# A third weight tile, and weights asked for earlier, in a two-layer decoder trunk on one core

## The chip, the cores and the metric

One core of a Trainium2 chip runs the whole program as one launch. The metric is the device time of one execution in microseconds. Before the change it is 1894.92 us, the median of 3 runs (1894.47 to 1899.17).

## The reference

The input is 512 tokens of width 1024 in float32. Two layers each do a half-weighted gated feed-forward step, a token mixer, and a second half-weighted feed-forward step; a final norm ends the program.

```python
def swiglu(x, w_gate, w_up, w_down):
    return (jax.nn.silu(x @ w_gate) * (x @ w_up)) @ w_down      # hidden width 2816

for i in range(DEPTH):                                          # 2 layers
    h = h + 0.5 * swiglu(rmsnorm(h, ffn_norm_a[i]), ffn_a_w_gate[i], ffn_a_w_up[i], ffn_a_w_down[i])
    m = rmsnorm(h, mix_norm[i])
    h = h + (mla_mixer(m, ...) if i % 2 == 0 else nsa_mixer(m, ...))
    h = h + 0.5 * swiglu(rmsnorm(h, ffn_norm_b[i]), ffn_b_w_gate[i], ffn_b_w_up[i], ffn_b_w_down[i])
return rmsnorm(h, final_norm)
```

The mixer of layer 0 is latent attention (`mla_mixer`): queries, keys and values come through low-rank projections, 16 heads, with a rotary part. The mixer of layer 1 is sparse attention (`nsa_mixer`): 16 heads in 4 groups; each token attends in a compressed branch (keys and values pooled over blocks of 32 tokens), a selected branch and a window branch, and the three outputs are summed with learned gates. All is causal.

## The kernel before, in words

Every matrix is split into a high and a low part (a copy in the faster matmul type, then source less copy), and a product is three matmuls: high x high, high x low, low x high (`mm3`, L161). So each slab of weights is loaded by SyncE's queue into a raw tile `wr`, copied by ScalarE into the high half of a weight tile `w`, and subtracted by VectorE, or in attention by GpSimd (`lo_pool`, L147 to L150), into the low half. `wslab` (L133) does all this; `wtiles` (L126) hands out the weight tiles, of which there are two in turn, and raw tiles are two as well. The high and low halves of a weight tile do not begin at its start: `wtiles` puts an offset of 0, 16 or 48 floats ahead of the high half and 0 or 32 more between the two, by the kind of use.

A pool's tiles lie in on-chip memory one behind the other, and the pools too: a scratch that the launch reserves, constants, the residual stream `h`, the normed activations (`x`, and `four` for tiles four times as wide), the weights (two weight tiles, a small tile, two raw tiles), a small pool, and then the pools of the current stage, feed-forward or attention.

The feed-forward stage (`ffn`, L369) does its first three hidden blocks plainly: gate and up products of 256-token halves (`plain`, L357, tiles `pg` and `pu`). The other 19 blocks form sums of weights and of activations and so need 7 products in place of 8 (`wsums` L309, `product` L348; tiles `px`, `pq`, `pg`, 256 wide). The down products (`pd`, 512 wide) run between them in units of three blocks, and the last one or two blocks (`tail`) at the end, where the next stage's norm is prepared. The norm's scale is applied late: gates and products are multiplied by a `row` that is computed from a sum of squares (`sumsq`, `norm_col`, `norm_bcast`) while the plain blocks run.

Latent attention (`mla`, L642) and sparse attention (`nsa`, L834) run a software pipeline over tiles of scores (`attend`, L569): scores on TensorE, softmax on VectorE and ScalarE, division by the sum on GpSimd (L772, L1091), transposes of the probabilities four tiles later, and the product with the values two or three tiles after that. Projections for later heads are cut into pieces and put into this pipeline by a table: `make(g, q, k, q2, c)` (L1190) gives the tile numbers at which the pieces of a group's first query, its keys, its second query, and the three steps of its compressed branch are issued. Of these three, `scores` forms the scores, `softmax` transposes them (`ptc`, L1041), normalises them, with the last scaling on GpSimd (`e`, L1053), and `turn` transposes them back (`ptc`, L1058).

A scheduler decides the order on each engine from the order of the code and priorities; each engine then works through its own list in order and waits on semaphores.

Of the kernel before, what the change touches and what calls it, by code (L numbers as in the profile page):

```python
# [18 lines left out]
P = 128  # L19
# [31 lines left out]
PAD = 16  # L51
TILES = 24
# [10 lines left out]
class Kern:  # L63
# [62 lines left out]
    def wtiles(self, kind="x"):  # L126

        t = self.first or self.wp.tile([P, 2048 + 3 * PAD], F32R, tag=f"w{self.nw % 2}", name="w")
        self.nw, self.first = self.nw + 1, None
        o, d = {"x": (0, 0), "act": (3 * PAD, 0), "half": (PAD, 2 * PAD)}[kind]  # L130
        return t[:, o : o + 1024], t[:, o + d + 1024 : o + d + 2048]
# [142 lines left out]
    def norm_col(self, n, s2, pool=False):  # L274
# [5 lines left out]
        return self.rsqrt_col(pc[:, 0:4], n, pool)  # L280
# [88 lines left out]
    def ffn(self, idx, gain_next, ap, tp):  # L369
        nc, a = self.nc, self.a  # L370
        self.scr, self.fp = (tp, "sq", 1), tp
        ah, al, ht, row = {}, {}, [], None
# [56 lines left out]

        gates = [self.bank("T", "pg") for _ in range(PLAIN)]  # L430
        for f, g in enumerate(gates):
            u = tu[f] = self.bank(("mm", "S")[f % 2], "pu")
            self.plain(idx, f, 0, g)
            if f == 1 and idx == 0:

                squares(0)
                tokens(3)
                squares(1)
            if f == 2:
                pb = self.norm_bcast(col)  # L440
                row = tp.tile([P, S], F32, tag="row", bufs=1, name="row")
                nc.scalar.activation(row, pb, AF.Copy)
                for e in range(2):
                    gate(e, gates[e])
                    act(e)
            self.plain(idx, f, 1, u)
            if f == 0 and idx:
                for c in self.late:
                    self.sumsq(self.h[c])
                col = self.norm_col(D, self.s2)  # L450
            elif f == 1 and idx == 0:
                squares(2)
                squares(3)
                col = self.rsqrt_col(sums, D)
            elif f == 2:
                gate(f, g)
                act(f)
            for p in (((0,), (1,), (2, 3)) if idx else ((0, 1), (2,), (3,)))[f]:
                self.combine(p)
# [182 lines left out]
    def mla(self, gain_next):  # L642
        nc, tc, a = self.nc, self.tc, self.a
        with ExitStack() as cx:
# [130 lines left out]
            def end(h):  # L775
# [58 lines left out]
    def nsa(self, gain_next):  # L834
        nc, tc, a = self.nc, self.tc, self.a
        with ExitStack() as cx:
# [18 lines left out]
            def pieces(src, done, more, nk=4):  # L855

                p, w = [], []

                def piece(k0):
                    if k0 == 0:  # L860
                        w.extend(self.wslab(src, (KC, P)))
                        p.append(self.mm_bank("pp"))
# [5 lines left out]
                return [partial(piece, k0) for k0 in range(0, KC, KC // nk)] + more  # L868

            def keys(g):  # L870
# [3 lines left out]
                def done(p):  # L874
                    tt.append(qp.tile([P, S], F32, tag="t", bufs=1, name="t"))
# [23 lines left out]
            def vals():  # L899

                ws = []

                def piece(j, kk):
                    if not ws:
                        ws.extend(self.wslab(a["nsa_w_v"][z], (4, 256), "half") for z in range(2))
# [9 lines left out]
                return [partial(piece, j, kk) for j in range(4) for kk in range(2)]  # L915

            def query(t2):
# [3 lines left out]
                def done(p):  # L921
                    tt.append(qp.tile([P, S], F32, tag="t", bufs=1, name="t"))
# [13 lines left out]
            with tc.tile_pool(name="cmp", bufs=1, reuse_waits="tile") as bp:  # L936
# [48 lines left out]
                for f in kf[:2]:  # L985
                    f()
# [5 lines left out]
                for f in kf[2:]:  # L992
# [149 lines left out]
            def end(h, z, br):  # L1142
# [12 lines left out]
                o, t = bank[m], tp.tile([P, S], F32, tag="p", bufs=6, name="ot")[0:64, :]  # L1155
# [15 lines left out]
            def w_o(c2):  # L1171

                w = []

                def piece(e):
                    if e == 0:
                        w.append(self.wslab(a["nsa_w_o"][0, c2], (2, 4, P), "act"))
                    self.w_o1(w[0], oh[:4], ol[:4], c2 + KP * e, e, False)

                return [partial(piece, e) for e in range(2)]  # L1180
# [153 lines left out]
```

## Time and profile before

| | |
|---|---|
| median of 3 runs | 1894.92 us |
| profiled execution | 1895.84 us, its span 1894.1 us |
| TensorE (PE) busy | 1865.5 us, 98% |
| weight loads into TensorE (PEld) | 1695.8 us, 90% |
| VectorE (DVE) busy | 1527.9 us, 81% |
| ScalarE (ACT) busy | 1088.9 us, 57% |
| GpSimd (POOL) busy | 244.7 us, 13% |
| granted TensorE clock, mean | 0.998 |
| read from memory | 178.96 MB, 96 GB/s over the span |

In the span's course, feed-forward runs from 0 to about 350 us, latent attention to about 550, feed-forward of both layers to about 1235, sparse attention to about 1530, and feed-forward to the end. Matmuls overlap each other, so the mean length of one (its latency) is longer than the distance between two starts; where a group's mean length rises, so does that distance. A list of waits names the engine's instruction, what released it, the total in us, how often and the longest. In a row of groups the numbers behind the first bar are busy us and mean ns, behind the second the idle time of the engine just before.

### The profile page before, as it was taken

To read this page: it belongs to the slowest core of one execution; us is meant where nothing else is said; L and a number is where in the kernel's file an instruction comes from. 1 tells how busy PE (TensorE), PEld (TensorE's weight loads), DVE (VectorE), ACT (ScalarE), POOL (GpSimd) and SP (SyncE) were. 2 spreads that over 40 slices of the span, in tenths; PEclk is the share of its full clock that TensorE was granted. 3 is DMA by queue.
4 is the path that set the end of the run, shared out by engine and by line. 5 is a ranking of instruction groups with operands and counts; after the bars stand their busy time and mean duration, and the time that the engine had idled before them with its cause. 6 is when DMAs were issued, how large, how long until landed. Compare 5 with 4: busy or idle time off the path is not lost.

```text
span 1894.1 us, 32916 instructions
## 1 busy us (share of the span) xinstructions
PE 1865.5 (98%) x12504; PEld 1695.8 (90%) x12504; DVE 1527.9 (81%) x2913; ACT 1088.9 (57%) x2024; POOL 244.7 (13%) x334
## 2 busy tenths in 40 slices
PE   8999999999999999999999999999989999999998
PEld 8999999878889999998999999888778889999997
DVE  8988886677778888886898878666978988888885
ACT  8555554478765555554654555436867865555553
POOL 0000000047710000000000000015656600000000
PEclk9999999999999999999999999999999999999999
DMA  6433331311132333322333332143121133333321
GB/s 237 131 101 100 102 100 41 112 53 46 60 132 90 124 101 101 102 79 86 130 124 108 105 105 75 55 141 102 51 71 64 43 115 111 111 107 104 104 77 67
DMA packets 75902, 183.26 MB, mean 97 GB/s; under 512 B 9040, under 2 KB 37072, under 8 KB 75744
## 3 DMA queue, kind: packets, MB, share of 16 engines
q1 hardware_dynamic: 72800, 176.39, 29.4%
q10 hardware_dynamic: 2944, 4.77, 0.7%
q8 instruction: 98, 1.61, 0.4%
q14 instruction: 60, 0.49, 0.1%
HBM read 178.96 MB, written 2.16 MB: 96 GB/s over the span
## 4 chain that ended last, share of the span: by engine, by line
PE 86%; DVE 6%; ACT 4%; POOL 2%; issue 1%; DMA 0%; POOLq 0%; SPq 0%; DVEq 0%; ACTq 0%
PE pd L164 8%; PE pd L165 8%; PE pd L163 8%; PE px L353 5%; PE px L354 5%; PE px L355 5%; PE pg L353 4%; PE pg L354 4%; PE pg L355 4%; PE pq L354 3%; PE pq L353 3%; PE pq L355 3%; PE o L1139 1%; PE po L164 1%; PE po L165 1%; PE po L163 1%
## 5 line engine op out<-in xcount | busy, mean ns | idle before, releaser
L164 PE MATMUL pd<-al,wd 128*128 128x512 f32 x576 | 225.3, 391 | 0.0
L163 PE MATMUL pd<-ah,wd 128*128 128x512 f32 x576 | 224.9, 390 | 0.0
L165 PE MATMUL pd<-ah,wd 128*128 128x512 f32 x576 | 224.6, 390 | 0.0
L172 DVE TENSOR_TENSOR w<-wr,w 128x1024 fp32r<-128x1024 f32 x72 | 88.2, 1224 | 123.9 <-ACT w L171 123.9
L353 PE MATMUL px<-four,wh 128*128 128x256 f32 x608 | 168.8, 278 | 0.6 <-ACT pg L478 0.6
L355 PE MATMUL px<-four,wl 128*128 128x256 f32 x608 | 168.0, 276 | 0.0
L354 PE MATMUL px<-four,wh 128*128 128x256 f32 x608 | 167.9, 276 | 0.0
L353 PE MATMUL pq<-four,wh 128*128 128x256 f32 x608 | 167.8, 276 | 0.0
L354 PE MATMUL pq<-four,wh 128*128 128x256 f32 x608 | 167.8, 276 | 0.0
L355 PE MATMUL pq<-four,wl 128*128 128x256 f32 x608 | 167.8, 276 | 0.0
L144 ACT ACTIVATE w<-wr 128x1024 fp32r<-128x1024 f32 (+5 forms) x120 | 100.7, 845 | 113.7 <-issue 25.7
L171 ACT ACTIVATE wd<-wdr 128x384 fp32r<-128x384 f32 x192 | 99.3, 519 | 98.5 <-ACT wd L171 59.1
L402 DVE SCALAR_TENSOR_TENSOR h<-pd,h 128x512 f32<-128x512 f32 x216 | 147.9, 685 | 6.9 <-PE pd L165 6.8
L165 PEld LDWEIGHTS pd<-ah,wd 128*128 128x128 f32 x576 | 108.2, 188 | 22.8
L163 PEld LDWEIGHTS pd<-ah,wd 128*128 128x128 f32 x576 | 108.1, 188 | 20.5
L164 PEld LDWEIGHTS pd<-al,wd 128*128 128x128 f32 x576 | 108.1, 188 | 19.7
L172 DVE TENSOR_TENSOR wd<-wdr,wd 128x384 fp32r<-128x384 f32 x192 | 106.1, 555 | 16.3 <-ACT wd L171 15.6
L146 DVE TENSOR_TENSOR w<-wr,w 128x1024 fp32r<-128x1024 f32 (+4 forms) x81 | 80.7, 998 | 45.1 <-ACT w L144 44.8
L640 ACT ACTIVATE p<-p,small 128x512 f32<-128x512 f32 (+2 forms) x192 | 106.5, 557 | 17.2 <-DVE small L639 14.2
L353 PEld LDWEIGHTS px<-four,wh 128*128 128x128 f32 x608 | 114.1, 188 | 2.5 <-ACT pg L478 1.9
L353 PEld LDWEIGHTS pq<-four,wh 128*128 128x128 f32 x608 | 114.2, 188 | 0.1
L354 PEld LDWEIGHTS pq<-four,wh 128*128 128x128 f32 x608 | 114.1, 188 | 0.1
(354 smaller groups left out, 6106.3 us busy)
## 6 DMA issues: line engine op xcount, KB each, us to landing
wr<-in_w_gu SPq DMA_DIRECT2D x96, 512.0 KB, 3.3
ru<-in_w_gu SPq DMA_DIRECT2D x76, 512.0 KB, 4.2
wdr<-in_w_down SPq DMA_DIRECT2D x192, 192.0 KB, 2.4
wr<-in_w_down SPq DMA_DIRECT2D x24, 256.0 KB, 2.6
wr<-in_mla_w_o SPq DMA_DIRECT2D x8, 512.0 KB, 3.4
wr<-in_nsa_w_q SPq DMA_DIRECT2D x8, 512.0 KB, 3.3
th<-btab_d SPq DMA_DIRECT2D x16, 256.0 KB, 3.5
wr<-in_nsa_w_o SPq DMA_DIRECT2D x8, 512.0 KB, 3.6
```

The costliest lines, as they stand in the source:

```text
L144: self.copied = nc.scalar.activation(wh[:, m], raw[:, m], AF.Copy)
L146: nc.vector.tensor_tensor(wl[:, m], raw[:, m], f32v(wh[:, m]), op=ALU.subtract)
L163: mm(out, wh, xh, start=first, stop=False)
L164: mm(out, wh, xl, start=False, stop=False)
L165: return mm(out, wl, xh, start=False, stop=last)
L171: nc.scalar.activation(hi, src, AF.Copy)
L172: (nc.gpsimd if pool else nc.vector).tensor_tensor(lo, src, f32v(hi), op=ALU.subtract)
L353: mm(out, wh[:, p], xh, start=first and p == 0, stop=False, skip_group_check=True)
L354: mm(out, wh[:, p], xl, start=False, stop=False, skip_group_check=True)
L355: mm(out, wl[:, p], xh, start=False, stop=last and p == KP - 1, skip_group_check=True)
L402: nc.vector.scalar_tensor_tensor(self.h[c], p, 0.5, self.h[c], op0=ALU.mult, op1=ALU.add)
L640: nc.scalar.activation(p_sb[:, :n], p_sb[:, :n], AF.Exp, bias=nm, scale=-1.0, accum_out=sm)
```

## The change

Six things are changed together.

- The scratch that the launch reserves becomes 1,024 bytes per partition (it was 16,384 in the built program), and weight tiles become three in turn.
- In sparse attention the load of a weight slab becomes an entry of its own in the table, `make` and the calls of `at` get a tile number for it, and most are 2 to 4 tiles ahead of the first piece. The compressed branch's second transposes (`turn`) move from tile 21 or 22 to 25. Two scratch tiles (`t`, `ot`) get room of their own.
- In latent attention the low parts of the first two heads' queries and of the last output are subtracted by VectorE in place of GpSimd.
- In the feed-forward the last blocks' down weights use the tiles of the weight sums (`fr`, `fh`, `fl`) in place of `wr` and `w`.
- From the second feed-forward on, the gates of the first two blocks are issued ahead of the third block's gate product in place of behind it.
- There, the last two sums of squares and the norm's small steps get a higher priority (`URGENT`).

```diff
-        t = self.first or self.wp.tile([P, 2048 + 3 * PAD], F32R, tag=f"w{self.nw % 2}", name="w")
+        t = self.first or self.wp.tile([P, 2048 + 3 * PAD], F32R, tag=f"w{self.nw % 3}", name="w")
...
+        def spread():
+            pb = self.norm_bcast(col)
+            nc.scalar.activation(row, pb, AF.Copy)
+            for e in range(2):
+                gate(e, gates[e])
+                act(e)
...
+            if f == 2 and idx:
+                spread()
             self.plain(idx, f, 0, g)
+            if f == 2 and idx == 0:
+                spread()
...
             if f == 0 and idx:
-                for c in self.late:
-                    self.sumsq(self.h[c])
-                col = self.norm_col(D, self.s2)
+                with self.tc.high_priority(URGENT):
+                    for c in self.late:
+                        self.sumsq(self.h[c])
+                col = self.norm_col(D, self.s2, URGENT)
...
             p = self.mm_bank("pd")
-            down(p, self.wslab(a["w_down"][idx, c, :, tail * P :], (NF - tail, P), "act"), tail, NF)
+            raw = tp.tile([P, D], F32, tag="fr", bufs=3, name="wdr")[:, : (NF - tail) * P]
+            nc.sync.dma_start(raw, a["w_down"][idx, c, :, tail * P :])
+            w = [t[:, : (NF - tail) * P].rearrange("p (k c) -> p k c", c=P) for t in self.sum_tiles(1024)]
+            self.split(raw.rearrange("p (k c) -> p k c", c=P), *w)
+            down(p, w, tail, NF)
...
-                self.split(t, qh, ql, pool=True)
+                self.split(t, qh, ql, pool=h > 1)
...
-                    self.split(o32[0], hi, lo, pool=True)
+                    self.split(o32[0], hi, lo, pool=h + 1 < H)
...
+                def load():
+                    w.extend(self.wslab(src, (KC, P)))
+
                 def piece(k0):
                     if k0 == 0:
-                        w.extend(self.wslab(src, (KC, P)))
                         p.append(self.mm_bank("pp"))
...
-                    tt.append(qp.tile([P, S], F32, tag="t", bufs=1, name="t"))
+                    tt.append(qp.tile([P, S], F32, tag="t", bufs=2, name="t"))
...
-                o, t = bank[m], tp.tile([P, S], F32, tag="p", bufs=6, name="ot")[0:64, :]
+                o, t = bank[m], tp.tile([64, S], F32, tag="ot", bufs=1, name="ot")
...
-            make(1, (0, 1, 3, 5, 6, 7), (13, 14, 15, 17, 18, 19), (7, 8, 9, 11, 13, 14), (16, 18, 21))
-            make(2, (0, 1, 3, 4, 5, 6), (4, 5, 7, 8, 9, 10), (9, 10, 11, 12, 13, 14), (16, 18, 21))
-            at(2, vals(), 12, 13, 14, 15, 16, 17, 19, 20)
-            make(3, (0, 1, 3, 4, 5, 6), (5, 7, 8, 9, 10, 11), (9, 10, 11, 12, 13, 14), (16, 18, 22))
-            at(3, w_o(0) + w_o(1), 13, 15, 17, 20)
-            at(4, w_o(2) + w_o(3), 3, 8, 14, 19)
+            make(1, (0, 1, 2, 3, 5, 6, 7), (11, 13, 14, 15, 17, 18, 19), (5, 7, 8, 9, 11, 13, 14), (16, 18, 25))
+            make(2, (-2, 0, 1, 3, 4, 5, 6), (2, 4, 5, 7, 8, 9, 10), (6, 9, 10, 11, 12, 13, 14), (16, 18, 25))
+            at(2, vals(), 9, 11, 12, 13, 14, 15, 16, 17, 19, 20)
+            make(3, (-4, 0, 1, 3, 4, 5, 6), (2, 5, 7, 8, 9, 10, 11), (6, 9, 10, 11, 12, 13, 14), (16, 18, 25))
+            at(3, w_o(0) + w_o(1), 11, 13, 15, 14, 17, 20)
+            at(4, w_o(2) + w_o(3), 1, 3, 8, 10, 14, 19)
...
-    nc = bacc.Bacc("TRN2", target_bir_lowering=False, num_devices=1)
+    nc = bacc.Bacc("TRN2", target_bir_lowering=False, num_devices=1, dynamic_dma_scratch_size=1024)
```

How the order on the engines moves, at three places. First TensorE in sparse attention, where the second transposes of the third group's compressed branch stand (`s`: scores of a tile, `pt`: transposes of its probabilities, `ptc`: the second transposes, `o`: the product with the values). Before:

```order
L1080 MATMUL s<-four 128x512
L1081 MATMUL s<-four 128x512
L1114 MATMUL pt<-ident,p 128x128 x4
L1080 MATMUL s<-four,q 128x384
L1058 MATMUL ptc_15985<-ident,e 128x128 x4
L1081 MATMUL s<-four,q 128x384
L1147 MATMUL o<-four,vcm_14128 128x256 x2
```

And with the change, 28 rows further down:

```order
L1117 MATMUL s<-four,q 128x512
L1118 MATMUL s<-four,q 128x512
L1129 MATMUL pt<-ident,p 128x128 x4
L164 MATMUL pp<-x,w 128x512
L1073 MATMUL ptc_16109<-ident,e 128x128 x4
L165 MATMUL pp<-x,w 128x512
```

The `ptc` transposes leave the place ahead of the value products `o` and now stand among the pieces `pp` of the next group's query.

Second, SyncE's queue in the same group, around the two slabs of value weights (`wr<-in_nsa_w_v`; `cb` and `th` are tables of the relative bias). Before:

```order
L141 DMA wr<-in_nsa_w_q 128x1024
L1029 DMA cb<-btab_d 32x512 x4
L1097 DMA th<-btab_d 128x512
L141 DMA wr<-in_nsa_w_v 128x1024
L1097 DMA th<-btab_d 128x512 x3
L141 DMA wr<-in_nsa_w_v 128x1024
```

With the change:

```order
L142 DMA wr<-in_nsa_w_q 128x1024
L142 DMA wr<-in_nsa_w_v 128x1024
L1044 DMA cb<-btab_d 32x512 x4
L1112 DMA th<-btab_d 128x512
L142 DMA wr<-in_nsa_w_v 128x1024
L1112 DMA th<-btab_d 128x512 x3
```

The first slab passes the compressed branch's table and one bias table, the second passes three bias tables.

Third, GpSimd at the start of latent attention's pipeline (`w<-wr`: low part of a weight slab, `<-tq`: low part of a head's query, `p<-p`: division of a tile's probabilities). Before:

```order
L150 TENSOR_TENSOR w<-wr,w 128x384 x2
L172 TENSOR_TENSOR four<-tq,four 128x512
L172 TENSOR_TENSOR four<-tq,q 128x512
L172 TENSOR_TENSOR q<-tq,four 128x512
L150 TENSOR_TENSOR w<-wr,w 128x512 x2
L772 TENSOR_SCALAR p<-p,small 128x512
```

With the change:

```order
L151 TENSOR_TENSOR w<-wr,w 128x384 x2
L151 TENSOR_TENSOR w<-wr,w 128x512 x2
L151 TENSOR_TENSOR w<-wr,w 128x384
L173 TENSOR_TENSOR q<-tq,four 128x512
L784 TENSOR_SCALAR p<-p,small 128x512
```

Two query splits are gone from GpSimd's list, and a value slab (two instructions) and one more query slab stand ahead of the first division.

More of the change, by code (lines that the diff above doesn't have):

```diff
@@ L51 @@
 PAD = 16
+URGENT = 400
 TILES = 24
@@ L272, in rsqrt, with norm_col @@
             nc.vector.scalar_tensor_tensor(y, t, 1.5, y, op0=ALU.add, op1=ALU.mult)
-    def norm_col(self, n, s2, pool=False):
+    def norm_col(self, n, s2, urgent=0):
         nc = self.nc
@@ L279, in norm_col @@
             nc.tensor.matmul(pc[:, i : i + 1], s2[:, i * P : (i + 1) * P], f32v(self.ones)[:, 0:1], start=True, stop=True)
-        return self.rsqrt_col(pc[:, 0:4], n, pool)
+        with self.tc.high_priority(urgent) if urgent else nullcontext():
+            return self.rsqrt_col(pc[:, 0:4], n)
     def rsqrt_col(self, s, n, pool=False):
@@ L371, in ffn @@
         self.scr, self.fp = (tp, "sq", 1), tp
-        ah, al, ht, row = {}, {}, [], None
+        ah, al, ht = {}, {}, []
         tg, tu, units = {}, {}, []
@@ L427, in ffn @@
                 tokens(t)
+        def spread():
[4 more added lines that the diff above has]
+                act(e)
+        row = tp.tile([P, S], F32, tag="row", bufs=1, name="row")
         gates = [self.bank("T", "pg") for _ in range(PLAIN)]
@@ L438, in ffn @@
                 squares(1)
[L439 to L445, printed above, removed]
             self.plain(idx, f, 1, u)
             if f == 0 and idx:
-                for c in self.late:
-                    self.sumsq(self.h[c])
-                col = self.norm_col(D, self.s2)
+                with self.tc.high_priority(URGENT):
+                    for c in self.late:
+                        self.sumsq(self.h[c])
+                col = self.norm_col(D, self.s2, URGENT)
             elif f == 1 and idx == 0:
@@ L866, in piece @@
                         done(p[0])
-                return [partial(piece, k0) for k0 in range(0, KC, KC // nk)] + more
+                return [load] + [partial(piece, k0) for k0 in range(0, KC, KC // nk)] + more
             def keys(g):
@@ L901, in vals, with load @@
                 ws = []
+                def load(z):
+                    ws.append(self.wslab(a["nsa_w_v"][z], (4, 256), "half"))
                 def piece(j, kk):
-                    if not ws:
-                        ws.extend(self.wslab(a["nsa_w_v"][z], (4, 256), "half") for z in range(2))
                     if kk == 0:
@@ L914, in piece @@
                         values(1, j, p)
-                return [partial(piece, j, kk) for j in range(4) for kk in range(2)]
+                return [partial(load, z) for z in range(2)] + [partial(piece, j, kk) for j in range(4) for kk in range(2)]
             def query(t2):
@@ L921, in done @@
                 def done(p):
-                    tt.append(qp.tile([P, S], F32, tag="t", bufs=1, name="t"))
+                    tt.append(qp.tile([P, S], F32, tag="t", bufs=2, name="t"))
                     nc.vector.scalar_tensor_tensor(tt[0], p, 0.125, row, op0=ALU.mult, op1=ALU.mult)
@@ L984, in nsa @@
                 kf = keys(0)
-                for f in kf[:2]:
+                for f in kf[:3]:
                     f()
@@ L991, in nsa @@
                 self.split(pk[:, : G * 32].rearrange("p (g n) -> p g n", g=G), at(kch), at(kcl))
-                for f in kf[2:]:
+                for f in kf[3:]:
                     f()
@@ L1173, in w_o, with load @@
                 w = []
+                def load():
+                    w.append(self.wslab(a["nsa_w_o"][0, c2], (2, 4, P), "act"))
                 def piece(e):
-                    if e == 0:
-                        w.append(self.wslab(a["nsa_w_o"][0, c2], (2, 4, P), "act"))
                     self.w_o1(w[0], oh[:4], ol[:4], c2 + KP * e, e, False)
-                return [partial(piece, e) for e in range(2)]
+                return [load] + [partial(piece, e) for e in range(2)]
             todo = {}
```

## The prediction

> **What bounds the kernel now.** I read the page first, then the list of TensorE's waits, then the windows by stage, then TensorE's groups by shape.
>
> ```profile
> span 1894.1 us, 32916 instructions
> PE 1865.5 (98%) x12504; PEld 1695.8 (90%) x12504; DVE 1527.9 (81%) x2913; ACT 1088.9 (57%) x2024; POOL 244.7 (13%) x334
> PE 86%; DVE 6%; ACT 4%; POOL 2%; issue 1%; DMA 0%; POOLq 0%; SPq 0%; DVEq 0%; ACTq 0%
> ```
>
> TensorE is busy for 98% of the span and holds 86% of the chain that ended last. It stands idle for 1894.1 - 1865.5 = 28.6 us; the list says for whom (total us, times, longest us):
>
> ```profile
> PE pg L365 <- ACT w L144: 5.7, 1, 5.7
> PE ptc L1058 <- POOL e L1053: 4.1, 4, 2.4
> PE pv L164 <- POOL w L150: 1.7, 2, 1.0
> PE pg L353 <- ACT pg L485: 1.2, 3, 0.8
> PE pv L163 <- ACT w L144: 0.7, 1, 0.7
> PE s L165 <- POOL four L172: 0.6, 1, 0.6
> PE po L164 <- POOL ol L172: 0.6, 1, 0.6
> PE pp L165 <- POOL w L150: 0.6, 1, 0.6
> PE px L353 <- ACT pg L478: 0.6, 3, 0.2
> PE pt L594 <- POOL p L772: 0.5, 1, 0.5
> ```
>
> The 5.7 us are the start, before the first weights are there; the change leaves them. What is left for it to win are small waits behind POOL and ACT. The windows (length, then busy time and count of PE, PEld, DVE, ACT, POOL, then the granted clock) say where TensorE has slack:
>
> ```profile
> 25.00:300.00 275.00, 274.74 (x2004) 257.62 (x2003) 239.60 (x375) 150.22 (x244) 0.00 (x0) 1.00 0.34 107
> 350.00:550.00 200.00, 195.70 (x1041) 164.00 (x1040) 142.93 (x406) 136.52 (x326) 96.30 (x120) 1.00 0.21 65
> 1300.00:1525.00 225.00, 216.69 (x1219) 181.09 (x1218) 188.66 (x600) 176.02 (x441) 139.00 (x183) 0.99 0.20 63
> ```
>
> A feed-forward stretch (25 to 300) has 0.3 us idle: there only the pace of the matmuls counts. Latent attention (350 to 550) has 4.3 us, sparse attention (1300 to 1525) 8.3 us.
>
> **The waits that the change removes.** In sparse attention the second transposes wait for POOL's scaling of the same tile, which stands behind a weight split:
>
> ```profile
> 1407.09 2.54 POOL L150 TENSOR_TENSOR w<-wr,w 128x512 fp32r<-128x512 f32 x2
> 1410.24 1.05 POOL L1053 TENSOR_TENSOR e<-e,small 128x512 f32<-128x512 f32 x1
> 1411.27 1.53 POOL L1091 TENSOR_SCALAR p<-p,small,gat 128x512 f32<-128x512 f32 x2
> ```
>
> Three of the four transposes move 3 or 4 tiles down; a tile is 225 us / 96 = 2.3 us, so they come 7 to 9 us later, more than the longest wait of 2.4. The one ahead of the loop stays (estimate 0.4): 4.1 - 0.4 = 3.7 us. What needs their result starts 9 tiles behind them, so nothing becomes late. The two slabs of value weights are now asked for 3 and 2 tiles ahead of use, with a third weight tile to hold them: the 1.7 + 0.7 = 2.4 us of `pv` go. On SP's queue they pass a compressed-score table and up to four bias tables; a slab of this size lands within 3.3 us, so a table behind it comes at most that much later, and the tables are asked for a head ahead.
>
> ```profile
> wr<-in_nsa_w_q SPq DMA_DIRECT2D x8, 512.0 KB, 3.3
> ```
>
> The `pv` waits cost more than they show, because the granted clock drops behind them:
>
> ```profile
> 1386.00:1389.50 3.50, 3.09 (x13) 3.06 (x14) 2.29 (x10) 1.77 (x7) 1.94 (x3) 0.51 0.46 152
> 1390.00:1393.00 3.00, 3.00 (x24) 2.86 (x23) 0.95 (x7) 0.46 (x3) 0.88 (x2) 1.00 0.01 3
> ```
>
> 3.5 us at 0.51 lose 3.5 x 0.49 = 1.7 us. With `pp` (0.6, a query's weights now loaded a tile ahead) sparse attention can win 3.7 + 2.4 + 1.7 + 0.6 = 8.4 us. The same splits (2.54 us a pair) still stand in POOL's queue, ahead of other tiles' scaling, and VectorE is busy for 188.66 of 225 us; so some waits return elsewhere. I take 7; bounds 3 and 8.4.
>
> In latent attention two query splits and the last output split go from POOL to VectorE:
>
> ```profile
> L172 POOL TENSOR_TENSOR ol<-o,oh 128x512 fp32r<-128x512 f32 x8 | 10.3, 1293 | 16.4 <-ACT oh L171 16.4
> L172 DVE TENSOR_TENSOR al<-tu,ah 128x512 fp32r<-128x512 f32 x88 | 60.3, 686 | 2.6 <-ACT ah L171 2.6
> ```
>
> Each is 1.29 - 0.69 = 0.6 us shorter there, and POOL has two fewer (2.6 us) ahead of the first probabilities; but a value and a query split come forward there (3 x 1.3 less a little), so those probabilities gain about 1 us. The waits of 0.6 (`s`), 0.5 (`pt`) and 0.6 (`po`) are 1.7 us: I take 1.5, bounds 0.5 and 1.7. VectorE is busy for 142.93 of 200 us there and has the room.
>
> In the feed-forward blocks the gates' work starts 48 matmuls (5.4 us at 0.113) earlier and the norm's small steps go ahead of the rest on VectorE. Waiting in front of it today are 1.2 + 0.6 = 1.8 us (`pg`, `px`): I take 0.9, bounds 0 and 1.8. The tail's weights use other buffers: same loads, same splits, and no wait on the tail today, so nothing. The copy `ot` and the second tile `t` cost nothing: the same instructions, hidden behind a busy TensorE.
>
> Together 7 + 1.5 + 0.9 = **9.4 us won**, between 3.5 and 11.9.
>
> **What the third weight tile moves.** It lies in the pool ahead of nearly everything. From the tile sizes: a weight tile is (2048 + 48) x 4 = 8384 bytes per partition, 32 x 256 + 192. The scratch reserved at the start shrinks by 15,360 bytes, 60 x 256. So the normed activations (`x`, `four`) keep their place modulo 256, all that lies behind the weight pool moves by 64 bytes against them, and the third tile begins 192 bytes off the grid of the other two. I call *distance* the start of the matmul's moving operand less the start of the stationary operand loaded during it, modulo 256 bytes, and counted it in the instruction lists of the two built programs. Of the 256-wide matmuls 116 have a distance of 0 or 128 before, and 5,844 after; the others have 64 or 192. In the feed-forward blocks it is 24 before, the last rows of the kernel, and 5,619 more after.
>
> What that costs, only the end of the kernel shows, away from attention. These are TensorE's groups from 1868 to 1886 us (mean ns behind the comma); all 256-wide ones there have 0 or 128, and of the 512-wide only `wl` has 128:
>
> ```profile
> L543 PE MATMUL pd<-wl,ah 128*128 128x512 f32 x11 | 4.3, 395 | 0.0
> L542 PE MATMUL pd<-wh,ah 128*128 128x512 f32 x11 | 4.3, 389 | 0.0
> L544 PE MATMUL pd<-w,al 128*128 128x256 f32 x4 | 1.1, 282 | 0.0
> L542 PE MATMUL pd<-wh,ah 128*128 128x256 f32 x4 | 1.1, 282 | 0.0
> L543 PE MATMUL pd<-wl,ah 128*128 128x256 f32 x4 | 1.1, 282 | 0.0
> L544 PE MATMUL pd<-wh,al 128*128 128x256 f32 x4 | 1.1, 280 | 0.0
> L543 PE MATMUL pd<-w,ah 128*128 128x256 f32 x4 | 1.1, 280 | 0.0
> L542 PE MATMUL pd<-w,ah 128*128 128x256 f32 x4 | 1.1, 277 | 0.0
> ```
>
> The page's row for the same width at 64 or 192, and one of the group that directly follows 512-wide matmuls:
>
> ```profile
> L353 PE MATMUL pq<-four,wh 128*128 128x256 f32 x608 | 167.8, 276 | 0.0
> L354 PE MATMUL px<-x,w 128*128 128x256 f32 x304 | 85.3, 281 | 0.0
> ```
>
> 280.5 on average against 276: 4.5 ns. That it is pace and not only latency, the starts tell (first and last of 24 there, and of 13 in a feed-forward block):
>
> ```profile
> 1882.97 0.28 PE L542 MATMUL pd<-w,ah 128*128 128x256 f32 x1
> 1885.68 0.28 PE L544 MATMUL pd<-wh,al 128*128 128x256 f32 x1
> 212.27 0.28 PE L353 MATMUL pq<-four,wh 128*128 128x256 f32 x1
> 213.63 0.28 PE L353 MATMUL px<-four,wh 128*128 128x256 f32 x1
> ```
>
> 2.71 / 23 = 117.8 ns against 1.36 / 12 = 113.3 ns: 4.5 again. Against it speaks `px<-x,w`: at 64 and 192 it has 281 too, so a run of 256-wide matmuls right behind 512-wide ones is slow for a while whatever the distance, and the last rows stand behind 512-wide ones. In the feed-forward blocks that passes within 12 matmuls, though (`pq` behind it is at 276); at the end it lasts through all 24. And the 512-wide `wl`, 395 against 389, has no such excuse. So I price 0 and 128 alike at 4.5 ns; bounds 0 (it is only the neighbours) and 6 (the 512-wide rows). The 362 `px<-x,w` among the 5,619 are slow already: 5,257 x 4.5 = **23.7 us lost**, between 0 and 32. The 512-wide ones that move (about 600, mostly to 64 or 192 in attention) lie between 0 and 6 ns, up to 3.6 us; nearest to the unsettled attention rows, where it hardly shows, I take 0.5.
>
> [...]
>
> **The sum.** The profiled execution took 1895.84 us, 1.7 around its span, and 0.9 over the median of 1894.92. 1895.8 - 9.4 + 23.7 + 0.5 = 1910.6; less 0.9: **1910 us**, slower. Its own range, with 3 to 6 ns, is 1902 to 1918.
>
> **Rivals.**
> - *Placement costs nothing* (28%). Then 1894.9 - 9.4 = 1885.5, with the gain's bounds 1883 to 1891: faster. For it: the slow `px<-x,w`, which needs no distance. Against: 24 slow in a row, and the 512-wide pair.
> - *Only 128 costs* (14%). The 512-wide rows at 0 stand at 389, so 0 may be free. 3,243 feed-forward matmuls have 128 (without `px<-x,w`): x 4.5 to 6 = 15 to 19 us; 1894.9 - 9.4 + 17 = 1902.5. Against: the end's 256-wide ones at 0 are as slow as those at 128.
> - *Only 0 costs* (9%): 2,014 x 4.5 = 9.1; 1894.6, no change.
> - *The change doesn't do what it says* (7%): placement is free, but POOL's splits, pulled forward, delay the probabilities as much as the moved waits gave. From 8 us of such delays on nothing is left: about 1895 to 1898.
>
> **How the numbers follow.** The forecast has the remaining 42%. Slower by over 0.3% (5.7 us, about what a measurement of this kernel can tell from no change): 0.42 + 0.14 + 0.02 of the last rival = 0.58. Faster: the first rival without its weak end, 0.25. No change: 0.09 + 0.03 + 0.05 = 0.17. The range must reach the first rival and the forecast's upper part: 1884 to 1916.
>
> **What would show it.** Right: the groups `pq<-four,wh` and `px<-four,wh` go from 276 to about 280 ns and the feed-forward stretches grow by 1.5% or so, while `ptc` and `pv` leave the list of waits and the granted clock stays at 1.0 through sparse attention, which shrinks by 5 to 8 us. If `pq<-four,wh` stays at 276, the price is wrong and the first rival holds; if of `pq` the first of the three matmuls (all at 128) rises and the second (two thirds at 0) hardly, the second. If sparse attention does not shrink, the wins are wrong; what then waits, and for which POOL instruction, names the cause.

## The result, and the profile after

The change makes the kernel slower: 1911.78 us, the median of 4 runs (1911.48 to 1912.81), against 1895.37 us for 4 runs of the kernel before that were made beside them (1894.47 to 1899.17). The ratio is 1.0084, with a 95% interval of 1.0066 to 1.0101. The forecast was 1910. The profiled execution took 1911.48 us, its span 1909.7.

From the page of the changed kernel, span, busy times and the engines' shares of the chain of waits:

```profile
span 1909.7 us, 32847 instructions
PE 1889.4 (99%) x12504; PEld 1721.9 (90%) x12504; DVE 1538.4 (81%) x2916; ACT 1074.4 (56%) x2024; POOL 242.3 (13%) x331
PE 94%; ACT 2%; DVE 2%; issue 1%; POOL 0%; DMA 0%; SPq 0%; DVEq 0%; POOLq 0%; ACTq 0%
```

TensorE's share of the chain rises from 86 to 94%. It stands idle for 20.3 us where it was 28.6, and yet the span is 15.6 us longer: the same 12,504 matmuls keep it busy for 23.9 us more. The windows say in which stage. The five stretches are feed-forward, latent attention, two feed-forwards, sparse attention, feed-forward (length, then busy time and count of PE, PEld, DVE, ACT, POOL, the granted clock, DMA share, GB/s). Before:

```profile
0.00:346.10 346.10, 340.10 (x2420) 317.30 (x2421) 286.41 (x451) 191.57 (x310) 0.20 (x4) 1.00 0.36 117
346.10:560.80 214.70, 210.40 (x1105) 176.16 (x1104) 156.82 (x425) 145.49 (x339) 96.30 (x120) 1.00 0.22 70
560.80:1235.80 675.00, 674.59 (x4857) 631.12 (x4857) 559.63 (x876) 358.86 (x580) 2.01 (x5) 1.00 0.32 101
1235.80:1543.10 307.30, 298.69 (x1654) 251.49 (x1653) 240.52 (x687) 209.96 (x493) 146.14 (x206) 0.99 0.24 74
1543.10:1894.10 351.00, 341.72 (x2473) 319.71 (x2471) 284.51 (x478) 182.98 (x303) 0.00 (x0) 1.00 0.32 104
```

And after:

```profile
0.00:352.10 352.10, 346.11 (x2420) 323.77 (x2421) 291.05 (x454) 189.52 (x312) 0.20 (x4) 1.00 0.37 119
352.10:567.90 215.80, 211.37 (x1106) 176.31 (x1105) 159.15 (x426) 144.81 (x339) 91.94 (x117) 1.00 0.20 65
567.90:1256.20 688.30, 688.30 (x4858) 645.41 (x4857) 566.13 (x879) 353.00 (x580) 2.13 (x6) 1.00 0.32 101
1256.20:1553.60 297.40, 295.66 (x1654) 249.91 (x1653) 236.66 (x684) 208.49 (x492) 148.01 (x205) 1.00 0.24 75
1553.60:1909.70 356.10, 348.00 (x2473) 326.53 (x2471) 285.38 (x477) 178.62 (x302) 0.00 (x0) 0.99 0.31 99
```

Feed-forward loses 6.0 + 13.3 + 5.1 = 24.4 us, sparse attention wins 9.9, latent attention loses 1.1: together 15.6. The loss is pace, in the groups that the prediction had named. After:

```profile
L355 PE MATMUL px<-four,wh 128*128 128x256 f32 x608 | 171.7, 282 | 0.2 <-ACT pg L486 0.2
L355 PE MATMUL pq<-four,wh 128*128 128x256 f32 x608 | 170.9, 281 | 0.0
L356 PE MATMUL pq<-four,wh 128*128 128x256 f32 x608 | 170.5, 280 | 0.0
L356 PE MATMUL px<-x,w 128*128 128x256 f32 x304 | 84.9, 279 | 0.0
```

These stood at 276 to 278 ns before; `px<-x,w`, at 279 to 281 before, did not rise. The pace proper is the time from one start to the next. For the 256-wide matmuls that follow each other, matched with the addresses of the built program, it is 113.9 ns (4,023 at distance 64) and 114.1 (3,456 at 192) before; after, 118.7 (2,265 at 0) and 118.6 (3,363 at 128), and 115.0 and 114.4 for those left at 64 and 192.

From the list of TensorE's waits after (total us, times, longest):

```profile
PE pg L367 <- ACT w L145: 5.8, 1, 5.8
PE s L164 <- DVE small L651: 1.7, 5, 0.7
PE pb L293 <- DVE small L273: 0.7, 1, 0.7
PE s L166 <- DVE four L173: 0.5, 1, 0.5
PE ptc L1073 <- POOL e L1068: 0.3, 1, 0.3
```

`ptc` fell from 4.1 to 0.3 us, and `pv`, `pp` and `po` are gone. New or longer are waits for VectorE, all three in latent attention: scores `s` behind the row maxima (L651) and behind a query split, `pb` behind the norm's small steps.

### The profile page after: what moved, and what is told of

Its sections match the earlier page's. It is cut to its first block, busy times and chain, and to the rows that moved or that the text cites. A ratio compares the mean times of both kernels' runs of the same rounds, so it can differ in the third digit from the quotient of the medians.

```text
span 1909.7 us, 32847 instructions
## 1 busy us (share of the span) xinstructions
PE 1889.4 (99%) x12504; PEld 1721.9 (90%) x12504; DVE 1538.4 (81%) x2916; ACT 1074.4 (56%) x2024; POOL 242.3 (13%) x331
## 4 chain that ended last, share of the span: by engine, by line
PE 94%; ACT 2%; DVE 2%; issue 1%; POOL 0%; DMA 0%; SPq 0%; DVEq 0%; POOLq 0%; ACTq 0%
PE pd L165 8%; PE pd L166 8%; PE pd L164 8%; PE px L355 6%; PE px L357 6%; PE px L356 6%; PE pg L355 4%; PE pg L357 4%; PE pq L357 4%; PE pq L355 4%; PE pg L356 4%; PE pq L356 4%; PE o L1154 2%; PE pt L1129 2%; PE po L164 2%; PE po L165 2%
## 5 line engine op out<-in xcount | busy, mean ns | idle before, releaser
L355 PE MATMUL px<-four,wh 128*128 128x256 f32 x608 | 171.7, 282 | 0.2 <-ACT pg L486 0.2
L356 PE MATMUL px<-four,wh 128*128 128x256 f32 x608 | 171.1, 281 | 0.0
L355 PE MATMUL pq<-four,wh 128*128 128x256 f32 x608 | 170.9, 281 | 0.0
L173 DVE TENSOR_TENSOR wl<-s,wh 128x512 fp32r<-128x512 f32 x76 | 52.5, 691 | 146.9 <-ACT wh L172 146.9
L356 PE MATMUL pq<-four,wh 128*128 128x256 f32 x608 | 170.5, 280 | 0.0
L145 ACT ACTIVATE w<-wr 128x1024 fp32r<-128x1024 f32 (+5 forms) x96 | 85.5, 897 | 87.8 <-issue 17.5
L172 ACT ACTIVATE wh<-s 128x512 fp32r<-128x512 f32 x76 | 47.9, 631 | 152.0 <-PE px L356 144.3
L355 PEld LDWEIGHTS px<-four,wh 128*128 128x128 f32 x608 | 115.0, 189 | 0.4 <-ACT pg L486 0.4
L357 PEld LDWEIGHTS px<-four,wl 128*128 128x128 f32 x608 | 115.1, 189 | 0.0
L356 PEld LDWEIGHTS px<-four,wh 128*128 128x128 f32 x608 | 114.8, 189 | 0.0
L355 PEld LDWEIGHTS pq<-four,wh 128*128 128x128 f32 x608 | 114.6, 188 | 0.0
```

Source lines behind the costliest of these rows:

```text
L145: self.copied = nc.scalar.activation(wh[:, m], raw[:, m], AF.Copy)
L172: nc.scalar.activation(hi, src, AF.Copy)
L173: (nc.gpsimd if pool else nc.vector).tensor_tensor(lo, src, f32v(hi), op=ALU.subtract)
L355: mm(out, wh[:, p], xh, start=first and p == 0, stop=False, skip_group_check=True)
L356: mm(out, wh[:, p], xl, start=False, stop=False, skip_group_check=True)
L357: mm(out, wl[:, p], xh, start=False, stop=last and p == KP - 1, skip_group_check=True)
```

## The experiments

All times below belong to one profiled run of each kernel (stretches and span) and to the median of its timed runs; "ratio" is to the kernel before, run beside it on the same chip.

| kernel | feed-forward | latent | sparse | span | median us | ratio |
|---|---|---|---|---|---|---|
| before | 1372.1 | 214.7 | 307.3 | 1894.1 | 1895.4 | |
| the change | 1396.5 | 215.8 | 297.4 | 1909.7 | 1911.78 | 1.0084 |
| after_realigned | 1371.9 | 214.8 | 297.2 | 1883.9 | 1885.67 | 0.9943 |
| before_shift192 | 1394.9 | 215.8 | 307.2 | 1917.9 | 1919.22 | 1.0118 |
| before_shift64 | 1396.9 | 214.9 | 308.1 | 1919.9 | 1921.21 | 1.0130 |
| before_shift128 | 1371.6 | 215.6 | 307.6 | 1894.8 | 1897.28 | 1.0004 |
| before_shift32 | 1395.8 | 215.8 | 306.2 | 1917.8 | 1921.07 | 1.0131 |
| before_shift224 | 1400.8 | 215.8 | 307.8 | 1924.5 | 1925.93 | 1.0158 |
| before_low64 | 1390.5 | 214.6 | 307.4 | 1912.4 | 1914.98 | 1.0107 |
| realigned_old_table | 1372.3 | 214.9 | 301.8 | 1889.1 | 1890.54 | 0.9972 |
| realigned_turn_only | 1370.6 | 215.8 | 297.2 | 1883.6 | 1885.43 | 0.9943 |
| realigned_q_on_gpsimd | 1372.4 | 217.5 | 297.2 | 1887.1 | 1887.50 | 0.9952 |
| two_tiles | 1370.9 | 213.7 | 302.6 | 1887.1 | 1889.02 | 0.9966 |
| third_tile_sparse_only | 1371.6 | 213.6 | 297.0 | 1882.2 | 1883.98 | 0.9936 |

**Is it the placement?** The first kernel takes the misplacement out of the change, the next three put it into the kernel before, in different amounts and with the order of every engine as it was.

```diff
# after_realigned: on the changed kernel
-        t = self.first or self.wp.tile([P, 2048 + 3 * PAD], F32R, tag=f"w{self.nw % 3}", name="w")
+        t = self.first or self.wp.tile([P, 2048 + 3 * PAD + 16 * (self.nw % 3 == 1)], F32R, tag=f"w{self.nw % 3}", name="w")
# before_shift192, 64, 128 (and 32, 224 below): on the kernel before, with N = 48, 16, 32 (8, 56) floats of 4 bytes
-        t = self.first or self.wp.tile([P, 2048 + 3 * PAD], F32R, tag=f"w{self.nw % 2}", name="w")
+        t = self.first or self.wp.tile([P, 2048 + 3 * PAD + N * (self.nw % 2)], F32R, tag=f"w{self.nw % 2}", name="w")
```

> The changed kernel with 64 bytes added to the second weight tile and nothing else: the third weight tile and all pools behind it come back to the places modulo 256 that they had before the change; the order on every engine is that of the changed kernel. Theory of the prediction (placement costs 4.5 ns a 256-wide matmul at distance 0 or 128): the loss goes and the gain of 9.4 us stays, 1895.4 - 9.4 = 1886 us, between 1883 and 1891. Rival (placement is free, the 16 us come from the moved work): it stays at about 1911.8 us.

> The kernel before with 192 bytes added to its second weight tile and nothing else: the pools behind the weights stand as in the changed kernel, with no other edit. Of the 256-wide matmuls 1,653 then have distance 0 and 3,199 have 128, against 118 and 4 before. Theory of the prediction: 4,730 x 4.5 ns = 21.3 us, so 1895.4 + 21.3 = 1916.7 us. Rivals: placement is free, 1895 us; only 128 costs, 3,195 x 4.5 = 14.4, 1910 us; only 0 costs, 1,535 x 4.5 = 6.9, 1902 us.

> The kernel before with 64 bytes added to its second weight tile: 3,297 of the 256-wide matmuls have distance 0 and 1,555 have 128, the counts of the shift by 192 bytes with 0 and 128 exchanged. Theory of the prediction: the same 21.3 us, 1916.7 us. Rivals: placement is free, 1895 us; only 128 costs, 1,551 x 4.5 = 7.0, 1902 us; only 0 costs, 3,179 x 4.5 = 14.3, 1910 us.

> The kernel before with 128 bytes added to its second weight tile: the pools move as before, but the 256-wide matmuls stay at 64 or 192 (102 at 0 and 20 at 128); of the 512-wide ones 784 have 128, against 93. Theory of the prediction: nothing for the 256-wide, 691 x 6 ns = 4.1 us for the 512-wide, 1899.5 us at most and 1895 at least. Rival (any move of the pools against the weights costs, whatever the distance): about 1917 us as with 64 and 192 bytes.

64 bytes of padding turn the changed kernel from 1911.8 into 1885.67 us (ratio 0.9943, 0.993 to 0.9955). Of the 25.8 us by which the span shrinks, 24.6 lie in the feed-forward stretches, where the same groups are back at 276 ns:

```profile
L355 PE MATMUL pq<-four,wh 128*128 128x256 f32 x608 | 167.8, 276 | 0.0
L356 PE MATMUL pq<-four,wh 128*128 128x256 f32 x608 | 167.8, 276 | 0.0
```

The kernel before, shifted by 192 bytes and otherwise untouched, loses 22.7 us; by 64 bytes, 24.7; by 128 bytes nothing (0.9995 to 1.0014). So it is the placement and no moved work, it is not the shift as such, and 0 and 128 cost alike: "only 128" would have given 1910 and 1902 us for the two shifts, "only 0" 1902 and 1910, and both took 1919 to 1921. The 512-wide matmuls that the shift by 128 bytes puts at distance 128 do not show in the whole time (0.8 us, within the interval nothing), but they are not free: matched one by one with the kernel before, 739 of them take 4.1 ns longer from start to start, 3.0 us together, and small differences elsewhere in the two executions made up for most of it.

**Which distances?** The shift by 32 bytes gives 32 and 160, the one by 224 bytes 96 and 224.

> The kernel before with 32 bytes added to its second weight tile: of the 256-wide matmuls 3,154 then have distance 32 and 1,551 have 160; 106 have 0 or 128; the rest 64, 192 or 224. It asks for the shape of the rule. If a conflict is one of 64-byte pieces (32 touches the piece at 0, 160 the one at 128), about 4,700 x 4.8 ns = 22.6 us are lost: 1918 us. If only starts exactly 0 or 128 apart conflict: 1895 us. If half of each row conflicts: about 1907 us. The prediction says nothing of 32 and 160.

> The kernel before with 224 bytes added to its second weight tile: 3,146 of the 256-wide matmuls have distance 96 and 1,555 have 224, 106 have 0 or 128, the rest 64 or 192. Shifted by 32 bytes (distances 32 and 160) it took 1921.1 us. Theory (of the multiples of 32 only 64 and 192 are fast): about 1918 to 1921 us. Rival (a matmul is slow where its piece begins in the first half of a 128-byte row as seen from the other: 0, 32, but not 64, 96): 1895 to 1897 us.

They cost 25 and 30 us. With the shifts above, all eight multiples of 32 have been seen; 64 and 192 are the only fast ones. The pieces of 64 bytes are refuted as a reason: in pieces counted from a tile's start, 96 is of the same piece as 64, and it is slow (119.5 ns from start to start; 224, of the same piece as 192, has 120.0). The idea of half rows falls with it. From these two kernels, the same group as above:

```profile
L354 PE MATMUL pq<-four,wh 128*128 128x256 f32 x608 | 171.1, 281 | 0.0
```

```profile
L354 PE MATMUL pq<-four,wh 128*128 128x256 f32 x608 | 172.4, 284 | 0.0
```

One rival these runs leave standing. In the feed-forward blocks, up to the 24 at the kernel's end, every 256-wide matmul takes its moving operand from `x` or `four`, and their tiles begin at a multiple of 256 bytes in all the kernels here. So its distance says no more than where the stationary operand begins (distance 64 is place 192, and the other way round), and whether the pair or that place alone sets the pace is not shown for them. Two small groups of the kernel before point opposite ways: the last 24 are slow at place 192 with distance 0 and 128 (117.8 ns), which speaks for the pair, and `pv<-w,x` in sparse attention is slow at place 0 with distance 64 and 192 (117.9 and 116.7 ns), which speaks for the place; both stand in runs of 12 to 24, and `px<-x,w` shows that such runs can be slow at any distance. For the 512-wide ones it is the pair: 698 of them have a stationary operand in a weight tile, which stays, and a moving operand behind it, which the shifts move; matched one by one with the kernel before (distance 0) they take 0.9 ns longer at 64 and 4.8 to 5.0 longer at 32, 192 and 224.

**Is each slow matmul slow by itself?** The prediction took a matmul's distance to the operand loaded during it; the distance to its own stationary operand gives nearly the same counts. To separate them, only the low halves of the weight sums were moved, by 64 bytes.

```diff
-        return hi, self.fp.tile([P, n + 2 * PAD], F32R, tag="fl", bufs=3, name="wl")[:, 2 * PAD :]
+        return hi, self.fp.tile([P, n + 2 * PAD], F32R, tag="fl", bufs=3, name="wl")[:, PAD : PAD + n]
...
-                lo = pool.tile([P, n + 2 * PAD], F32R, tag=tag[1], bufs=bufs, name="wl")[:, 2 * PAD :]
+                lo = pool.tile([P, n + 2 * PAD], F32R, tag=tag[1], bufs=bufs, name="wl")[:, PAD : PAD + n]
```

> The kernel before with the low halves of the weight sums 64 bytes further forward in their tiles, and nothing else: of each three matmuls of a product (high with high, high with low, low with high) only the one that uses the low half as its stationary operand has its own distance at 0 or 128, and only the one ahead of it (high with low) has a distance of 0 or 128 to the operand loaded during it; 1,516 matmuls in either count. So the time is the same, 1895.8 + 1,516 x 4.8 ns = 1903.1 us; what is told apart is which of the two is slow. Theory by the distance of the prediction: the second of three has a pace of 118 to 119 ns and the third 114. Rival (the distance to its own stationary operand): the third 118 to 119, the second 114. If both are slow, it is the neighbourhood, and 1910 us.

```profile
L353 PE MATMUL pq<-four,wh 128*128 128x256 f32 x608 | 169.5, 279 | 0.0
L354 PE MATMUL pq<-four,wh 128*128 128x256 f32 x608 | 170.3, 280 | 0.0
L355 PE MATMUL pq<-four,wl 128*128 128x256 f32 x608 | 170.9, 281 | 0.0
```

All three of a triple are slow, also the first, which stands at 64 by either count. From start to start the three of `pq` take 116.2, 117.3 and 118.9 ns, against 113.5, 113.3 and 113.3 before (starts that had to wait left out). The kernel loses 19.0 us where 1,516 matmuls at 4.8 ns would have made 7.3: 12.5 ns for each one out of place. So a run of matmuls slows as a whole, and one in three out of place costs most of what all three would (19.0 us against 1,516 x 3 x 4.8 = 21.8). Neither of the two distances alone explains that; the 4.5 ns of the prediction hold where nearly all are out of place, and are no price of a single one.

**Where the gain in sparse attention comes from.** On the realigned kernel the table of sparse attention was set back, first all of it, then all but the moved second transposes (tile 25).

```diff
# realigned_old_table: loads at the first piece again, and
-            make(1, (0, 1, 2, 3, 5, 6, 7), (11, 13, 14, 15, 17, 18, 19), (5, 7, 8, 9, 11, 13, 14), (16, 18, 25))
+            make(1, (0, 1, 3, 5, 6, 7), (13, 14, 15, 17, 18, 19), (7, 8, 9, 11, 13, 14), (16, 18, 21))
...
# realigned_turn_only: the same, with (16, 18, 25) in the three calls of make
```

> after_realigned with the table of sparse attention as it was before: loads at the first piece, second transposes of the compressed branch at tile 21 or 22; third weight tile, the two scratch tiles and all other edits stay, and so do all places in memory. Theory (the table does it): the waits ptc (4.1 us) and pv (2.4 us) and the half-clock stretch come back, and of the 10.1 us by which the sparse stretch shrank at least 8 are lost again: 1894 to 1896 us. The prediction's term gives 7: 1892.7 us. Rival (the third weight tile alone ends the pv waits, since a load need not wait for a tile): only ptc comes back, 1885.7 + 4 = 1890 us, and no pv in the list of waits.

> realigned_old_table with the compressed branch's second transposes at tile 25, and nothing else of the table. Theory: ptc falls from about 4.1 to 0.4 us, so 3.7 us less than realigned_old_table, and pv with the half-clock stretch stays: about 1891.5 us. Rival (the half-clock stretch hangs on the ptc waits too): the clock stays at 1.0 and it is within 2 us of after_realigned, 1887.5 us.

With the old table the `pv` waits do not come back. TensorE's list of waits in that stretch is, in full,

```profile
PE ptc L1070 <- POOL e L1065: 3.2, 3, 2.4
PE sc L1045 <- DVE small L651: 0.5, 1, 0.5
PE pkc L1001 <- issue: 0.3, 1, 0.3
```

so the third weight tile alone ends them: the stretch is 301.8 us and not 307.3. The moved transposes alone then bring the other 4.6 us, to 297.2, what the whole table gives (1.7 of the 4.6 are a half-clock stretch behind a `ptc` wait, on which more below); asking for the weights earlier adds nothing to that (1885.43 against 1885.67 us). For both kernels the rival on record held and the theory fell. The crossing was run as well, the change with two tiles:

```diff
-        t = self.first or self.wp.tile([P, 2048 + 3 * PAD], F32R, tag=f"w{self.nw % 3}", name="w")
+        t = self.first or self.wp.tile([P, 2048 + 3 * PAD], F32R, tag=f"w{self.nw % 2}", name="w")
```

> The changed kernel with two weight tiles in turn, not three; the new table, the moved transposes and all other edits stay, and the pools behind the weights stand at 64 or 192 again. Sparse attention took 307.2 us before, 301.8 with three tiles and the old table, 297.2 with three tiles and the new one or with three tiles and the moved transposes alone. Theory (the third tile ends the pv waits, asking earlier does nothing, since a load has to wait for a free tile): the pv waits and the half-clock stretch stay, ptc goes: about 302 us for the stretch, 1890 us in all. Rival (the prediction: asking earlier ends them): 297 to 298 us, 1886 us. In latent attention, where the third tile lets GpSimd's weight split run ahead, two tiles should give 213.5 to 214.5 us against 214.9.

```profile
PE pv L165 <- POOL w L151: 1.5, 2, 1.0
PE pv L164 <- ACT w L145: 0.6, 1, 0.6
PE pp L166 <- POOL w L151: 0.6, 1, 0.6
```

A slab asked for earlier still waits for a free tile: `pv` keeps 2.1 of its 2.4 us, and the stretch has 302.6 us, as foreseen.

**Why latent attention won nothing.** The same run shows the splits on VectorE as the prediction priced them, and a stretch of 213.7 us. VectorE with two tiles (the two query splits and the first row maximum):

```profile
401.44 0.69 DVE L173 TENSOR_TENSOR four<-tq,four 128x512 fp32r<-128x512 f32 x1
402.05 0.68 DVE L173 TENSOR_TENSOR four<-tq,q 128x512 fp32r<-128x512 f32 x1
403.25 0.68 DVE L651 CUSTOM_DVE_ANT_0 p<-s,mask 128x512 f32<-128x512 f32 x1
```

With three tiles (after_realigned), VectorE, and the split on GpSimd at that time:

```profile
401.83 1.37 DVE L173 TENSOR_TENSOR four<-tq,four 128x512 fp32r<-128x512 f32 x1 [0.52 <-ACT four L172]
403.12 1.77 DVE L173 TENSOR_TENSOR four<-tq,q 128x512 fp32r<-128x512 f32 x1
405.42 0.67 DVE L651 CUSTOM_DVE_ANT_0 p<-s,mask 128x512 f32<-128x512 f32 x1
```

```profile
401.36 2.99 POOL L151 TENSOR_TENSOR w<-wr,w 128x512 fp32r<-128x512 f32 x2 [3.15 <-ACT w L145]
```

With two tiles that pair of GpSimd's begins at 404.49, behind VectorE's splits; the third tile lets it begin at 401.36, beside them. The splits then take 1.37 and 1.77 us, not 0.69, and the first row maximum comes 2.2 us later, for which `s` waits. GpSimd's pair is longer beside them too: 2.99 us, 2.55 with two tiles. Why is not shown, and not every row of VectorE's is longer beside GpSimd: in the kernel before, a `tq` product takes 0.69 us from 402.54 on, while GpSimd splits a query (402.46 to 403.75). Leaving the queries on GpSimd is no way out:

```diff
# realigned_q_on_gpsimd: on after_realigned
-                self.split(t, qh, ql, pool=h > 1)
+                self.split(t, qh, ql, pool=True)
```

> after_realigned with the first two heads' query splits of latent attention back on GpSimd; the last output split stays on VectorE. Latent attention took 214.8 us before and takes 214.8 in after_realigned, though the three waits behind GpSimd (0.6, 0.5, 0.6) are gone. Theory (the two splits on VectorE took 1.37 and 1.77 us beside a GpSimd split, not 0.69, and so the first row maxima came 2.3 us later, for which scores wait 0.7): the waits s behind GpSimd (0.6) and pt (0.5) come back, s behind VectorE's maxima falls from 1.6 to about 0.3, po stays away: 214.2 us for the stretch. Rival (the prediction: VectorE's splits win 1 us): the stretch grows to 215.8 us. In the whole time the two are 1884.5 to 1885.1 and 1886.7 us.

```profile
PE s L166 <- POOL four L173: 2.2, 1, 2.2
PE pb L293 <- DVE small L273: 1.6, 1, 1.6
```

The stretch grows to 217.5 us, and the wait behind GpSimd is 2.2 us where it was 0.6 before: with three tiles the weight pair stands ahead of the query splits there (402.91 against 405.39), in the kernel before it stood behind them (405.23 against 401.23). Of the 2.7 us between the two, 0.7 are `pb`, which is 0.2 with two tiles and 0.7 to 1.8 with three, whoever splits the queries. Another 1.7 are 3.41 us at half clock from 407.80 on, behind that wait, which not every execution need have (last section). So theory and rival were both wrong on the sign or the size, and the place was right: the move to VectorE is worth some 2 us where the clock drops and a few tenths where it doesn't, and only makes good what the third tile spoils in this stage.

**A faster version.** So the third tile was confined to the stage that gains by it.

```diff
# third_tile_sparse_only: on after_realigned
-        t = self.first or self.wp.tile([P, 2048 + 3 * PAD + 16 * (self.nw % 3 == 1)], F32R, tag=f"w{self.nw % 3}", name="w")
+        t = self.first or self.wp.tile([P, 2048 + 3 * PAD + 16 * (self.nw % self.wn == 1)], F32R, tag=f"w{self.nw % self.wn}", name="w")
# wn is 2 from setup on, and in nsa:
+        self.wn = 3
```

> after_realigned, but weight tiles are two in turn until sparse attention begins and three from there on; nothing else. Theory (the third tile is of use in sparse attention alone, and in latent attention lets GpSimd's weight splits run ahead of the first query splits): latent attention takes 213.7 us as in two_tiles, sparse attention 297.2 as in after_realigned, the feed-forward blocks the same: 1.2 us less than after_realigned, about 1884.5 us, the fastest of all. Rival (the 1.2 us in latent attention were variation from run to run): 214.5 us or more, and 1885.7 us.

Its latent and sparse attention:

```profile
346.90:560.50 213.60, 210.22 (x1105) 176.19 (x1104) 156.62 (x426) 144.09 (x338) 92.11 (x117) 1.00 0.20 66
1235.80:1532.80 297.00, 295.42 (x1653) 250.25 (x1652) 236.74 (x684) 208.22 (x492) 147.78 (x205) 1.00 0.24 75
```

1883.98 us (1883.51 to 1884.58; ratio 0.9936, 0.9923 to 0.995): 11.2 us below the kernel before, 27.8 below the change. That it beats after_realigned by the 1.2 us of latent attention is shown by the stretch, not by the ratios, whose intervals overlap.

## Why the prediction was right, point by point

- **The loss** (23.7 us for 5,257 256-wide matmuls, 0.5 for 512-wide). Right in place, cause and size: 24.4 us in the feed-forward stretches, 26.1 between the change and its realigned form. The 512-wide term was too small: matched with the realigned kernel, 341 matmuls at 192 take 3.7 ns longer and 185 at 64 take 2.0, some 1.7 us. The rows at the kernel's end that carried the price were the right ones to read, and the 512-wide pair (395 against 389) was the right reason to set aside the first rival. The step "the 362 `px<-x,w` are slow already" holds in sum (279 ns after, 281 before), though not one by one: those left at 64 and 192 became faster (a pace of 114.3 ns on average against 117.2 for all of them before), those at 0 and 128 slower (119.2), and for the first no run gives a reason. What was wrong is the form of the term, so many matmuls times 4.5 ns: *before_low64* shows the price to belong to the run of matmuls. It came out because in the changed kernel nearly all were misplaced together.
- **Sparse attention** (7 won, bounds 3 and 8.4). Too small and outside its bounds: 9.9 in the change, 10.1 realigned. Idle time there fell from 307.30 - 298.69 = 8.6 to 297.20 - 295.43 = 1.8 us, which is 6.8, and the half-clock stretch gave its 1.7; the other 1.6 lie in the matmuls' own busy time, which the sum did not have; where, was not traced further. The 1.7 us belong to single executions, as the last section shows. The discount of 1.4 for waits that return elsewhere was not needed. What failed is half of the reason given for `pv`: the prediction named the earlier request and a third tile to hold it; the tile alone ended those waits, and the request without it did not.
- **Latent attention** (1.5 won, bounds 0.5 and 1.7). Not borne out: 1.1 lost in the change, 0.1 realigned. The 1.0 between the two fits placement: the kernel before, shifted by 192 bytes with its order untouched, has the same 215.8 us there. The three waits did go; the splits were priced at 0.69 us from rows with GpSimd idle, and the change itself, by the third tile, put GpSimd's weight splits beside them. With two tiles the term is 1.0 us, inside its bounds.
- **Feed-forward** (0.9 won, bounds 0 and 1.8). Not seen. Kernels at 64 and 192 have 1372.1 and 1371.6 us with the old code, 1370.6 to 1372.4 with the new: nothing above what differs from run to run. `pg` and `px` waits of about 1 us come and go between runs of either code.
- **The sum.** -9.4 + 24.2 was forecast; by the span of the realigned kernel it came as -10.2 + 25.8. Behind the 10.2 stand errors that partly cancel (sparse attention 3.1 us more than forecast, latent attention 1.6 and feed-forward 0.7 less), and what is left of them cancels part of the larger loss. So 1910 against 1911.8 is closer than the terms deserve, and that is luck.
- **The rivals.** "Placement costs nothing" is refuted by both directions of the experiment: realigning alone brings the feed-forward stretches 24.6 us, shifting alone takes 22.8 and 24.8 from them. "Only 128" and "only 0" fell by the two shifts. "The change doesn't do what it says" was true in part: most of the table does nothing, but in sparse attention no wait took the place of those removed; in latent attention the waits for VectorE did.
- **The signs** named ahead came: 276 to 280 and more in `pq` and `px`, feed-forward longer by 1.8%, `ptc` and `pv` off the list, the clock at 1.00 through sparse attention, and the first and second matmul of `pq` up alike (281 and 280).

## What to carry to other kernels

Where TensorE is the bound, a new buffer is also a shift of everything behind it: compare the places of moving and stationary operands modulo 256 before and after, and pad the new buffer until they are as they were; here 64 bytes were worth 26 us, more than twice what the rest of the change won. Look at what a third buffer releases, not only at what it was asked for: it ended the weight waits without any new order, and in another stage let one engine's work run into its neighbour's. And price a moved instruction by rows in which the neighbouring engine is as busy as it will be: here the two splits took 1.37 and 1.77 us on VectorE beside GpSimd's weight split, 0.69 and 0.68 without it.

## What the runs showed of the hardware that was not expected

Of the eight distances that are multiples of 32 bytes, 256-wide matmuls keep a pace of 113.7 to 115.6 ns at 64 and 192 only; at 0, 32, 96, 128, 160 and 224 they take 118 to 120 (kernels with whole pools shifted). The 512-wide ones differ: at distance 0 they have 228.6 ns, the best pace of theirs. Why a few misplaced operands slow their neighbours is open, as is which of the two distances matters, or whether for the 256-wide ones the stationary operand's place alone does.

The half clock in sparse attention is not tied to the `pv` waits. In the kernel before it followed them, and the longer `ptc` wait of 2.4 us went by without it. In realigned_old_table, without `pv` waits, it followed the same `ptc` wait and cost as much. Each such stretch lasts 3.41 us in the records of the granted clock, ten times in attention in the runs here (once in latent attention, the other times in sparse), and costs 3.41 x 0.5 = 1.7 us. Windows of that length, counted from its start, show how busy TensorE was ahead of it in the kernel before (TensorE's busy time is the second number, the clock third from the end; first the `pv` waits, then the `ptc` wait):

```profile
1382.67:1386.08 3.41, 1.36 (x7) 0.95 (x7) 2.34 (x8) 2.65 (x5) 3.38 (x4) 1.00 0.00 1
1386.08:1389.49 3.41, 3.08 (x13) 3.06 (x14) 2.21 (x9) 1.68 (x7) 1.86 (x3) 0.50 0.47 156
1406.56:1409.97 3.41, 2.41 (x19) 2.01 (x17) 3.34 (x13) 3.41 (x10) 3.41 (x4) 1.00 0.00 0
1409.97:1413.38 3.41, 2.04 (x15) 1.91 (x16) 2.09 (x7) 1.69 (x5) 2.83 (x4) 1.00 0.46 154
```

In realigned_old_table:

```profile
1406.01:1409.42 3.41, 1.47 (x12) 1.39 (x12) 2.23 (x7) 1.89 (x5) 3.38 (x5) 1.00 0.39 154
1409.42:1412.83 3.41, 3.41 (x15) 3.03 (x14) 1.61 (x5) 3.13 (x6) 1.66 (x2) 0.50 0.26 77
```

In the kernel before the `ptc` wait is divided between two windows in which TensorE was busy for 71 and 60%. Over the ten stretches, the window ahead had it busy for 35 to 51%; in the same runs no window of 56% or more was followed by one. A share that decides is not shown: at the end of the kernel before, a window with 45% (from 1884.42 us on) was followed by one at a clock of 1.00, and half clock came behind that next one, which has no matmul (from 1891.25 on); in the changed kernel it came behind a window with 28% (from 1904.04 on). Nor is a length of wait: before_shift32, with `ptc` and `pv` waits of 4.0 and 2.5 us, lost nothing to the clock in attention (mean over the span 0.999), and before_shift64, with 4.1 and 1.8, lost it twice (0.997). So the 1.7 us that the prediction took for the waits' price belongs to one execution. Busy time is the profile's, whose matmul ends are modelled.
